# Buffers taken ahead of their loads, and the squares of the memory moved, in a one-core decoder layer

## The chip, the cores and the metric

The kernel runs on one core of one Trainium2 chip, in one launch. The metric is the device time of an execution in microseconds (us); where several were timed, it is their median. The profile is that of one execution; its times start with its span.

## The reference

One layer of a hybrid decoder: 512 tokens of width 1024, and a memory of 256 tokens of the same width, all in float32.

```python
x = x + 0.5 * swiglu(rms_norm(x, norm_ffn1_w), ffn1_w_in, ffn1_w_out)      # inner width 2816
x = x + hybrid_mixer(rms_norm(x, norm_mix_w), ..., rel_bias, w_out_mix)    # 16 SSD heads in 4 groups beside 8 attention heads
x = x + memory_cross_attention(rms_norm(x, norm_cross_w), rms_norm(mem, norm_mem_w), w_cq, w_ck, w_cv, w_co)
x = x + 0.5 * swiglu(rms_norm(x, norm_ffn2_w), ffn2_w_in, ffn2_w_out)
return rms_norm(x, norm_final_w)
```

Three things in it concern the change. `rms_norm(mem, ...)` needs the sum of squares of each memory token. The attention heads add a bias that is looked up from `rel_bias` by the bucket of the distance of two tokens. The SSD heads end in a norm over each group of 256 channels.

## The kernel before

**Matmuls.** A float32 factor is split into a rounded part and the remainder (`wh` and `wl` for weights, names in `h` and `l` for activations); ScalarE makes the first (L155), VectorE the second (L156), and TensorE multiplies three pairs of parts. A weight tile `wr` comes by a transfer on SP's queue into one of six buffers, is split into one of three pairs of buffers, and is then multiplied. Some weight blocks are summed on the way: a transfer on POOL's queue adds a second block to a `wr` that has landed.

**The first feed-forward.** Both feed-forwards use a scheme of block products with sums (seven products where eight would be plain). The inner width is worked through in three thirds (`THIRDS`: 8, 8 and 6 tiles of 128). In each third, `ffn_quads` makes gate and up projections: a quad (`quad`, L240) computes two inner tiles by seven products and ends in the gated tile `th`. `block_tiles` then makes from `th` the block tiles `g` (`g11`, `s31`, `s24`, `g`), six large buffers and two small ones a quad. `out_blocks` (L1266) multiplies a third's tiles by the second weight matrix, again in seven products, `oa`, `oe` and `ob`. The first third has four quads' worth of tiles, the second four, the last three. The activations' block sums `xs` stay in their buffers through all of it.

**Buffers.** Nearly all tiles come from one pool: `s2` gives a large buffer (128 x 512, 55 of them) or, for tiles of at most 256 columns, a small one (16). A buffer that was used before can be written once all who used it are done.

**The order of the work.** The program is written by an `Order` object with a virtual clock `od.t`, which each matmul moves on by its own length and nothing else moves. Dense work (a list of generators) is emitted in turn; chains (`od.spawn`) are steps that are put in between when the virtual clock has reached their time, and each `yield n` in a chain asks for its next step `n` us of matmul time later. SP and POOL execute in the order so written. For TensorE, VectorE and ScalarE a planner orders the instructions by its own estimate of when each could start, with the order written as priority; `behind(...)` ties an instruction after another on its engine. The planner also gives each transfer of SP and ScalarE one of eight counters in turn; a transfer waits until the last one on its counter has landed.

**Around the change.** `ffn1` calls `at_out(ti)`, which is `beside`, when it begins with the output products of third `ti`:

```python
        if ti == 0:
            od.spawn(lambdas())
        elif ti == 1:
            od.spawn(memory_squares())
        elif ti == 2:
            od.spawn(prepare())
            od.spawn(memory_in(hm), 1.0)
```

`memory_squares` loads the memory by token (`memt`, four tiles, L1013) and squares them on ScalarE into `msq` (L1017). `prepare` loads the one-hot buckets `hot` (L609), multiplies them by `rel_bias` (`prel`), copies the result back into `hot` (L620) and sends it, on ScalarE's queue, to the table `rel_d` in device memory (L623), and from there to `rel_z` (`expand_bias`, L629). `memory_in` loads the memory by channel (`mem`, four tiles of two, L1024) and splits it into `hm` for the keys of the cross-attention (L159, L160). Right after the last third, x is transposed back (`pxf`), and the keys (`pck`) begin.

In the mixer, `group` runs once for each of the four SSD groups as a chain. Near its end it sums squares with TensorE (`pn`), takes the root on POOL (`ncol`, L357), halves it on VectorE (`rh`, L990), and after `W["gn"]` calls `row_of`, which builds two diagonal matrices on POOL (`ndiag`, L368). After `W["gr"]` a matmul with ones (`nrow`) makes the row by which `y` is multiplied.

Of the kernel before, what the change touches and what calls it, by code (L numbers as in the profile page):

```python
# [13 lines left out]
AF = mybir.ActivationFunctionType  # L14
# [3 lines left out]
P = 128  # L18
T = 512
D = 1024  # L20
KT = D // P
NF = 22
MEM = 256
# [6 lines left out]
NUM_BUCKETS = 32  # L30
# [5 lines left out]
LEAD = 4  # L36

W = {"h0": 3.4, "hs": 3.3, "hv": 2.08, "hp": 6.75}
W |= {"g0": 8.28, "gc": 0.75, "gx": 0.92, "gb": 2.59, "gs": 0.51, "gt": 2.0, "gd": 6.9, "gy": 0.38, "gq": 11.8, "gn": 5.0, "gr": 3.0}
W |= {"c0": 4.97, "cs": 3.0, "ct": 4.82}  # L40

SPLIT, AHEAD = 5, 2
# [58 lines left out]
def body(tc, a, dbg=None):  # L101
    nc = tc.nc
# [12 lines left out]
    def nm(s):  # L115
        uid[0] += 1
        return f"{s}_{uid[0]}"

    def s2(s, dt=F32, shape=(P, T)):
        if math.prod(shape[1:]) <= T // 2:  # L120
            return sp.tile(list(shape), dt, tag="s1", name=nm(s), bufs=NHALF)
        return sp.tile(list(shape), dt, tag="s2", name=nm(s))
# [4 lines left out]
    def small(s, n, bufs=None):  # L127
        return tiny.tile([P, n], F32, tag=s, name=nm(s), bufs=bufs)
# [4 lines left out]
    def aux(s, shape=(P, T)):  # L133
        return aux_p.tile(list(shape), F32, tag="aux", name=nm(s))
# [5 lines left out]
    last, start, last_sum, recent, newest, newest_mm = [], [], [], [], [], []  # L140
    V, S, G = nc.vector, nc.scalar, nc.gpsimd
    od = Order()

    def mm(out, w, x, start, stop):
        od.t += (1 if w.dtype == R32 else 4) * (x.free_size() + 8) / 2400
        newest_mm[:] = [nc.tensor.matmul(out, w, x, start=start, stop=stop).ins]  # L146
# [16 lines left out]
    def split(s, src, scale=None, half=False, n=T):  # L163
        if half:
            both = s2(s, R32, (P, 2, T // 2))
            hi, lo = both[:, 0], both[:, 1]
        else:
            hi, lo = s2(s + "h", R32, (P, n)), s2(s + "l", R32, (P, n))
        last[:] = [i.ins for i in split_into(hi, lo, src, scale)]
        return hi, lo  # L170
# [12 lines left out]
    @contextmanager  # L183
    def behind(ins):
        with ExitStack() as after:
            for i in ins:
                after.enter_context(tc.issue_after(i))
            yield

    H = T // 2  # L190
# [359 lines left out]
    def beside(ti):  # L550
        if ti == 0:
            od.spawn(lambdas())
        elif ti == 1:
            od.spawn(memory_squares())
        elif ti == 2:
            od.spawn(prepare())
            od.spawn(memory_in(hm), 1.0)
# [17 lines left out]

    od.spawn(st1.finish(rows=0.0), 18.0)
    od.add(ffn1(h1, wa_s, beside, square, fin1))


# [6 lines left out]
    def lambdas():  # L586
        lamv = cp.tile([P, 4, 64], F32, name="lamv")
        nc.sync.dma_start(lamv, a["lam"].partition_broadcast(P))
        yield 8.0
        lamp = small("lamp", 64, bufs=2)  # L590
        lsum = small("lsum", 2, bufs=1)
        for j in range(2):
            V.tensor_tensor(lamp, lamv[:, 2 * j, :], lamv[:, 2 * j + 1, :], ALU.mult)
            V.reduce_sum(lsum[:, j : j + 1], lamp, axis=AX.X)
        yield 4.0
        lexp = small("lexp", 2, bufs=1)
        G.tensor_tensor(lexp, euler[:, 0:1].to_broadcast([P, 2]), lsum, ALU.pow)
        yield 4.0
        V.tensor_tensor(nlam, lexp[:, 1:2], lexp[:, 0:1], ALU.subtract)
        V.tensor_scalar(nlam, nlam, -LAMBDA_INIT, None, ALU.add)  # L600
        V.tensor_scalar(wsub, par[:, C_SUBLN : C_SUBLN + 1], 1.0 - LAMBDA_INIT, None, ALU.mult)
        V.tensor_scalar(dskh, par[:, C_DSKIP : C_DSKIP + 8], 0.5, None, ALU.mult)

    def prepare():
        rel_sb = small("rel_sb", 8, bufs=1)[:NUM_BUCKETS]
        nc.sync.dma_start(rel_sb, a["rel_bias"])
        hot = [s2("hot", shape=(NUM_BUCKETS, H)) for _ in range(2)]
        for i in range(2):
            nc.sync.dma_start(hot[i], a["hot"][:, i * H : (i + 1) * H])  # L609
        rel_far = small("rel_far", 64, bufs=1)[:8]  # L610
        V.memset(rel_far, MASKED)
        yield 9.0
        prel = aux("prel", (8, T))
        for i in range(2):
            mm(prel[:, i * H : (i + 1) * H], rel_sb, hot[i], True, True)
        for c in range(T, RW, 64):
            S.dma_start(rel_d[:, c : c + 64], rel_far)
        yield 1.5
        for i in range(2):
            S.activation(hot[i][:8], prel[:, i * H : (i + 1) * H], AF.Copy, scale=-8.0)  # L620
        yield 2.0
        for i in range(2):
            S.dma_start(rel_d[:, i * H : (i + 1) * H], hot[i][:8])  # L623
        yield 6.0
        for hd in range(2):
            expand_bias(S, hd)

    def expand_bias(queue, hd):
        queue.dma_start(rel_z[hd, :, :RW], rel_d[hd : hd + 1].to_broadcast([P, RW]))  # L629
# [377 lines left out]

    msq = small("msq", 4, bufs=1)

    def memory_squares():  # L1010
        mt = [s2("memt") for _ in range(4)]
        for j in range(4):
            nc.sync.dma_start(mt[j], a["memt"][j])  # L1013
        yield 12.0
        for j in range(4):
            with behind(list(recent)):
                S.activation(mt[j], mt[j], AF.Square, accum_out=msq[:, j : j + 1])  # L1017
            yield 4.0

    def memory_in(dst):  # L1020
        mem = []
        for k in range(0, KT, 2):
            mem.append(s2("mem2", shape=(P, 2, MEM)))
            nc.sync.dma_start(mem[-1], a["memT"][k : k + 2].rearrange("k p m -> p k m"))  # L1024
        yield 9.0
        for k in range(KT):
            mk = mem[k // 2][:, k % 2]
            with behind(recent):
                dst.append(split("hm", mk, par[:, C_MEM + k : C_MEM + k + 1], True))
            yield 2.0  # L1030
        both = small("nboth", 4, bufs=2)[:, :2]
        V.tensor_tensor(both, msq[:, :2], msq[:, 2:], ALU.add)
        yield from st_mem.from_sums(both, 10.0)
# [477 lines left out]
```

## Time and profile before

| | |
|---|---|
| median of 3 runs | 1342.84 us (1339.92 to 1343.74) |
| the profiled execution | 1341.54 us, span 1339.8 us |
| granted TensorE clock, mean | 0.988 |
| instructions | 20126 |
| busy: TensorE, VectorE, ScalarE, POOL | 97%, 74%, 53%, 9% of the span |
| moved by transfers | 236.34 MB, mean 176 GB/s |

In the profile PE is TensorE's matmuls and PEld its weight loads, DVE is VectorE, ACT ScalarE, POOL GpSimd, SP the engine that issues most transfers; SPq or ACTq marks a queue's own work, issuing and waiting. L155 is line 155 of the kernel. A row of a timeline has start and length in us, engine, line, operation, output and inputs, count, and in brackets the idle time before it with what ended it. A row of waits has who waited, for whom, and then total, number and longest in us. In the tables by stretches each row has the stretch, its length, each engine's busy time with its instructions in brackets, the granted clock as a share of full speed, the busy share of the transfer engines, and GB/s.

### The profile page before, as it was taken

The page shows a single profiled execution, that of the slowest core. Times are in us where ns is not written, and L with a number is a line of the kernel's source. Part 1 is how long each engine was busy: PE and PEld are TensorE (multiplying, and loading weights), DVE is VectorE, ACT ScalarE, POOL GpSimd, SP SyncE. Part 2 cuts the span into 40 slices and gives each one's busy share as a digit, 9 for nine tenths or more (in the row PEclk, how much of TensorE's full clock was granted, in tenths as well). Part 3 has the DMA queues.
Part 4 walks back from the last instruction along what each step waited for, and adds up shares of the span by engine and source line. Part 5 has one row for each costly group of instructions (what it writes and reads, how often), then busy time and mean ns, then how long its engine had stood idle before and what let it go on. Part 6 is the DMA issues. An engine that isn't in the chain of part 4 may idle for free.

```text
span 1339.8 us, 20126 instructions
## 1 busy us (share of the span) xinstructions
PE 1303.0 (97%) x7724; PEld 1131.8 (84%) x7724; DVE 985.9 (74%) x1564; ACT 709.6 (53%) x1192; POOL 124.0 (9%) x143
## 2 busy tenths in 40 slices
PE   9999997999899999989999999999999999999996
PEld 7898996898697778777788878888889989989995
DVE  7988785787786577637867868645588877877886
ACT  6554553455564464526655547334456545554564
POOL 0001010000020001010110311120001100000001
PEclk9999998999899999999999999999999999999999
DMA  7658765775794634673375647766148876656662
GB/s 269 167 168 209 184 159 172 208 185 137 228 310 158 180 83 95 212 209 111 81 179 189 151 142 227 228 172 190 47 127 222 212 228 180 188 192 180 186 207 86
DMA packets 70129, 236.34 MB, mean 176 GB/s; under 512 B 8257, under 2 KB 9761, under 8 KB 69681
## 3 DMA queue, kind: packets, MB, share of 16 engines
q1 hardware_dynamic: 54352, 183.20, 40.7%
q0 software_dynamic: 12880, 44.62, 19.2%
q10 hardware_dynamic: 2800, 7.23, 1.5%
q8 instruction: 61, 1.00, 0.3%
q14 instruction: 36, 0.29, 0.1%
HBM read 232.87 MB, written 50.91 MB: 212 GB/s over the span
## 4 chain that ended last, share of the span: by engine, by line
PE 91%; DMA 3%; DVE 3%; ACT 2%; issue 1%; POOL 0%; ACTq 0%; SPq 0%; POOLq 0%; DVEq 0%
PE qb L240 12%; PE pm L146 9%; PE qe L240 8%; PE qa L240 8%; PE pxbc L146 7%; PE ob L1266 6%; PE oe L1266 4%; PE oa L1266 4%; PE pq L146 3%; PE pk L146 3%; PE pcq L146 3%; PE pz L146 3%; PE pv L146 3%; PE pck L146 2%; PE pcv L146 2%; PE pg L146 2%
## 5 line engine op out<-in xcount | busy, mean ns | idle before, releaser
L155 ACT ACTIVATE wh<-wr 128x1024 fp32r<-128x1024 f32 (+1 forms) x329 | 334.9, 1021 | 381.8 <-issue 63.1
L156 DVE TENSOR_TENSOR wl<-wr,wh 128x1024 fp32r<-128x1024 f32 (+1 forms) x329 | 385.4, 1174 | 159.7 <-ACT wh L155 157.0
L146 PE MATMUL pxbc<-hnh,wh 128*128 128x512 f32 x128 | 52.2, 408 | 0.0
L146 PE MATMUL pxbc<-hnh,wl 128*128 128x512 f32 x128 | 50.3, 393 | 0.0
L146 PE MATMUL pxbc<-hnl,wh 128*128 128x512 f32 x128 | 50.1, 392 | 0.0
L763 ACT ACTIVATE ec<-ec,mn 128x512 f32<-128x512 f32 (+3 forms) x64 | 35.5, 557 | 24.1 <-DVE mn L762 24.1
L240 PE MATMUL qe<-s31h,wl 128*128 128x256 f32 x152 | 43.1, 283 | 0.0
L240 PE MATMUL qa<-h11h,wh 128*128 128x256 f32 x152 | 43.1, 283 | 0.0
L240 PE MATMUL qb<-s24h,wh 128*128 128x256 f32 x152 | 43.0, 283 | 0.0
L240 PE MATMUL qb<-s24l,wh 128*128 128x256 f32 x152 | 43.0, 283 | 0.0
L240 PE MATMUL qb<-s24h,wl 128*128 128x256 f32 x152 | 43.0, 283 | 0.0
L240 PE MATMUL qa<-hmh,wh 128*128 128x256 f32 x152 | 43.0, 283 | 0.0
L240 PE MATMUL qa<-hml,wh 128*128 128x256 f32 x152 | 43.0, 283 | 0.0
L240 PE MATMUL qa<-hmh,wl 128*128 128x256 f32 x152 | 43.0, 283 | 0.0
L240 PE MATMUL qe<-s24h,wh 128*128 128x256 f32 x152 | 43.0, 283 | 0.0
L240 PE MATMUL qe<-s24l,wh 128*128 128x256 f32 x152 | 43.0, 283 | 0.0
L240 PE MATMUL qe<-s24h,wl 128*128 128x256 f32 x152 | 43.0, 283 | 0.0
L240 PE MATMUL qb<-hmh,wh 128*128 128x256 f32 x152 | 43.0, 283 | 0.0
L240 PE MATMUL qb<-hml,wh 128*128 128x256 f32 x152 | 43.0, 283 | 0.0
L240 PE MATMUL qb<-hmh,wl 128*128 128x256 f32 x152 | 43.0, 283 | 0.0
L240 PE MATMUL qa<-h11h,wl 128*128 128x256 f32 x152 | 43.0, 283 | 0.0
L240 PE MATMUL qa<-h11l,wh 128*128 128x256 f32 x152 | 43.0, 283 | 0.0
(448 smaller groups left out, 4190.8 us busy)
## 6 DMA issues: line engine op xcount, KB each, us to landing
wr<-in_f2q SPq DMA_DIRECT2D x44, 512.0 KB, 4.4
wr<-in_f1q SPq DMA_DIRECT2D x40, 512.0 KB, 4.5
wr<-in_f1b SPq DMA_DIRECT2D x30, 512.0 KB, 5.2
isum<-in_f2q SPq DMA_DIRECT2D x22, 512.0 KB, 5.9
wr<-isum SPq DMA_DIRECT2D x22, 512.0 KB, 4.8
wsum<-in_f2b SPq DMA_DIRECT2D x20, 512.0 KB, 5.9
wr<-wsum SPq DMA_DIRECT2D x20, 512.0 KB, 4.4
wr<-in_f1q POOLq DMA_DIRECT2D x16, 512.0 KB, 7.5
```

The lines of the kernel that those rows point to most:

```text
L146: newest_mm[:] = [nc.tensor.matmul(out, w, x, start=start, stop=stop).ins]
L155: S.activation(hi, src, AF.Copy),
L156: V.tensor_tensor(lo, src, hi.bitcast(F32), ALU.subtract),
L240: newest_mm[:] = [nc.tensor.matmul(out, a_[:, wc], b_, start=first and f == 0 and kp == 0 and j == 0, stop=kp == n - 1 and j == 2, skip_gr ...
L763: S.activation(ec[:, :n], ec[:, :n], AF.Exp, bias=mn, scale=-1.0, accum_out=sm[c][:, i : i + 1])
L1266: newest_mm[:] = [nc.tensor.matmul(ps, a_[:, ts], b_[:, ws], start=first and k == 0 and j == 0, stop=k == n - 1 and j == 2, skip_group_che ...
```

## The change

It has two parts. The first concerns the memory loads. `memory_squares` becomes `early`, still spawned at the second third's output products. It waits 40 us of matmul time, takes the four `memt` buffers, waits 20 more, loads them, and squares them 14 later, one each 1.0 (before: load at once, squares from 12 on, one each 4.0, tied behind the latest weight split; now not tied). It then takes the four buffers of `mem` and the two of `hot`, ahead of `memory_in` and `prepare`, which use them where they took them before, and drop them with `clear()`. The second part changes two distances in `group`: from the root to the diagonals ("gn") 5.0 becomes 1.5, and from the diagonals to the row's matmuls ("gr") 3.0 becomes 5.3.

```diff
-... "gq": 11.8, "gn": 5.0, "gr": 3.0}
+... "gq": 11.8, "gn": 1.5, "gr": 5.3}
...
         elif ti == 1:
-            od.spawn(memory_squares())
+            od.spawn(early())
...
     def prepare():
         rel_sb = small("rel_sb", 8, bufs=1)[:NUM_BUCKETS]
         nc.sync.dma_start(rel_sb, a["rel_bias"])
-        hot = [s2("hot", shape=(NUM_BUCKETS, H)) for _ in range(2)]
         for i in range(2):
             nc.sync.dma_start(hot[i], a["hot"][:, i * H : (i + 1) * H])
...
             S.dma_start(rel_d[:, i * H : (i + 1) * H], hot[i][:8])
+        hot.clear()
         yield 6.0
...
-    def memory_squares():
+    mem, hot = [], []
+
+    def early():
+        yield 40.0
         mt = [s2("memt") for _ in range(4)]
+        yield 20.0
         for j in range(4):
             nc.sync.dma_start(mt[j], a["memt"][j])
-        yield 12.0
+        yield 14.0
         for j in range(4):
-            with behind(list(recent)):
-                S.activation(mt[j], mt[j], AF.Square, accum_out=msq[:, j : j + 1])
-            yield 4.0
+            S.activation(mt[j], mt[j], AF.Square, accum_out=msq[:, j : j + 1])
+            yield 1.0
+        mem.extend(s2("mem2", shape=(P, 2, MEM)) for _ in range(KT // 2))
+        hot.extend(s2("hot", shape=(NUM_BUCKETS, H)) for _ in range(2))

     def memory_in(dst):
-        mem = []
         for k in range(0, KT, 2):
-            mem.append(s2("mem2", shape=(P, 2, MEM)))
-            nc.sync.dma_start(mem[-1], a["memT"][k : k + 2].rearrange("k p m -> p k m"))
+            nc.sync.dma_start(mem[k // 2], a["memT"][k : k + 2].rearrange("k p m -> p k m"))
         yield 9.0
...
             yield 2.0
+        mem.clear()
```

More of the change, by code (lines that the diff above doesn't have):

```diff
@@ L38 @@
 W = {"h0": 3.4, "hs": 3.3, "hv": 2.08, "hp": 6.75}
-W |= {"g0": 8.28, "gc": 0.75, "gx": 0.92, "gb": 2.59, "gs": 0.51, "gt": 2.0, "gd": 6.9, "gy": 0.38, "gq": 11.8, "gn": 5.0, "gr": 3.0}
+W |= {"g0": 8.28, "gc": 0.75, "gx": 0.92, "gb": 2.59, "gs": 0.51, "gt": 2.0, "gd": 6.9, "gy": 0.38, "gq": 11.8, "gn": 1.5, "gr": 5.3}
 W |= {"c0": 4.97, "cs": 3.0, "ct": 4.82}
```

## The prediction

> **What bounds the kernel now.** I read the page first, then TensorE's waits, then each feed-forward stage alone in the table by stretches, then what SP and ScalarE waited for there.
>
> ```profile
> span 1339.8 us, 20126 instructions
> ## 1 busy us (share of the span) xinstructions
> PE 1303.0 (97%) x7724; PEld 1131.8 (84%) x7724; DVE 985.9 (74%) x1564; ACT 709.6 (53%) x1192; POOL 124.0 (9%) x143
> ```
>
> ```profile
> PE oa L1266 <- ACT wh L155: 7.9, 3, 4.0
> PE oe L1266 <- ACT wh L155: 7.7, 2, 5.5
> ```
>
> TensorE is the bound, with 1339.8 - 1303.0 = 36.8 us idle. A change that leaves the matmuls alone can win only idle time and time at a lowered clock. The two largest waits, 15.6 us, are in `out_blocks` (L1266). The next table (stretch, its length, busy time of PE, PEld, DVE, ACT, POOL, granted clock, DMA share, GB/s) sets its three runs in the first feed-forward side by side: the thirds with four, four and three quads. The third row is the quads between the last two.
>
> ```profile
> 94.16:132.47 38.31, 38.31 (x170) 31.45 (x170) 33.11 (x40) 19.87 (x23) 3.44 (x4) 1.00 0.77 208
> 213.16:266.20 53.04, 44.14 (x172) 34.78 (x171) 33.81 (x39) 22.64 (x31) 4.26 (x5) 0.87 0.73 212
> 266.20:326.58 60.38, 60.38 (x505) 60.38 (x504) 49.53 (x58) 32.52 (x40) 5.12 (x6) 1.00 0.74 182
> 326.58:370.06 43.48, 35.85 (x134) 26.32 (x133) 30.85 (x45) 23.93 (x45) 1.74 (x2) 0.88 0.59 181
> ```
>
> The first two do the same matmuls. One takes 38.31 us without an idle moment, the other 53.04 with 8.90 idle and a mean clock of 0.87. So stage A (213 to 266) loses 53.04 - 38.31 = 14.7 us. Stage B (326 to 370) has three quads; a later third of that size shows each of its seven products:
>
> ```profile
> 1075.19 4.08 PE oa L1266 x18
> ```
>
> ```profile
> 332.14 1.02 PE L146 MATMUL prel<-hot,rel_sb 32*8 32x256 f32 x4
> ```
>
> Seven by 4.08 is 28.6; with `prepare`'s matmuls of 1.0 it is 29.6. Stage B loses 43.5 - 29.6 = 13.9 us. The quads lose nothing. Together 28.6 us are to be had, and why they are lost is in SP's own waits (from 189 to 217 us, then from 304 to 336) and in when its weight loads go out:
>
> ```profile
> SPq L1013 <- DVE qe L300: 14.8, 1, 14.8
> SPq L1013 <- DVE g11l L156: 8.0, 1, 8.0
> SPq L1013 <- DVE c L307: 2.5, 1, 2.5
> SPq L1247 <- DVE wl L156: 2.2, 1, 2.2
> SPq L1013 <- DVE s24l L156: 0.2, 1, 0.2
> ```
>
> ```profile
> SPq L1247 <- DMA rel_d<-hot: 17.2, 1, 17.2
> SPq L1024 <- DMA wr<-in_f1b: 5.3, 1, 5.3
> ```
>
> ```profile
> 78.97 33.80 SPq L1247 DMA_DIRECT2D wr<-in_f1b  x10
> ...
> 216.88 30.31 SPq L1247 DMA_DIRECT2D wr<-in_f1b  x10
> ...
> 313.51 36.43 SPq L1247 DMA_DIRECT2D wr<-in_f1b  x10
> ```
>
> SP issues in the order written. At L1013 (`memt`) it stood 14.8 + 8.0 + 2.5 + 0.2 = 25.5 us for buffers, released by the last quad's `u2`, `p5` and `s24` and by the block split that follows it, and A's ten remaining weight loads were behind it. In the clean third their first goes out at 78.97, 15.2 us ahead of the stage; in A at 216.88, 3.7 us after its start: 18.9 us late. The code's count agrees: the pool has 55 large buffers. At the end of a third of four quads it holds 24 for `xs` (six a pair), 24 for `g` (six a quad), one row, three copies of a quad and two unsplit sums: 54. Four `memt` do not fit. With three quads it is 48, and four more make 52.
>
> In B the loads begin at 313.51 in good time, but then one stands 17.2 us for the landing of `rel_d<-hot`, and the rest behind it. No data joins the two. SP's and ScalarE's transfers take eight counters in turn, and one waits for the last transfer on its counter; the order is the planner's, which thought the weights late since it held `hot` and `mem` behind the last quad's buffers. ScalarE shows the same order:
>
> ```profile
> 333.21 0.64 ACT L620 ACTIVATE hot<-prel 8x256 f32<-8x256 f32 x2 [0.26 <-PE prel L146]
> 333.61 0.63 ACTq L623 DMA_DIRECT2D rel_d<-hot  x2
> 335.27 1.22 ACTq L629 DMA_DIRECT2D rel_z<-rel_d  x2
> 336.53 0.63 ACT L155 ACTIVATE wh<-wr 128x512 fp32r<-128x512 f32 x1 [2.68 <-issue]
> ```
>
> The split that TensorE needs at 332 stands behind the bias work, though its load was out at 313.51.
>
> **The change, part by part.** *Memory by token.* Four loads, four squares and their buffers leave stage A. `early` takes buffers 40 us after its start (A's 38.3 and some 2 us of quads), loads at 60 and squares from 74. The pool is then far from full. SP no longer stands in front of A's weights; the clean third is the model, so A becomes 38.3. **Gain 14.7**, between 0 (SP stands as long elsewhere) and 14.7. What is late next in A is nothing: VectorE's 33.81 us stay beside the clean third's 33.11. In the quads the moved work costs:
>
> ```profile
> L1013 SPq DMA_DIRECT2D memt<-in_memt x4: 327/328/328, 204.9 to 216.5; - x4
> L1017 ACT ACTIVATE memt<-memt x4: 615/616/621, 235.1 to 251.2; 128x512 f32<-128x512 f32 x4
> ```
>
> SP spends 4 x 0.33 = 1.3 us, ScalarE 4 x 0.62 = 2.5 us where it is busy 32.5 of 60.4: hidden. Without that cover 2.5 us come back. The squares also lose their place behind the weight splits; one of 0.62 ahead of a split is covered by the spare `wh` buffers.
>
> *`mem` and `hot`.* The same six loads stay at the start of B, but their buffers were set aside in the last quad. SP loses L1024's wait of 5.3 us or part of it, and the planner sees loads and weights early: ScalarE gets B's split ahead of `hot`, and the counters that `rel_d<-hot` holds meet later transfers. Queued behind them on SP are B's ten loads and then the keys' weights. What is late next is VectorE: 30.85 us of work for 29.6 of matmuls.
>
> ```profile
> DVE th L449 <- ACT gate L447: 1.1, 1, 1.1
> DVE gate L446 <- PE qb L240: 0.7, 1, 0.7
> ```
>
> ```profile
> 369.41 1.43 DVE L1277 SCALAR_TENSOR_TENSOR x<-ob,col,x 128x512 f32<-128x512 f32 x2 [0.15 <-PE ob L1266]
> ```
>
> Its two waits at the start remain, and its last update, 1.4 us, falls after the last matmul: 30.85 + 1.1 + 0.7 - 1.4 = 31.3 us is its floor in B. I add some 1.7 for hand-overs and take 33 (an estimate): **gain 43.5 - 33 = 10.5**, between 0 (the old order stays) and 13.9 (memory splits slip behind the stage).
>
> What such a remainder does to the clock is one question more:
>
> ```profile
> 355.69 0.79 PE L1266 MATMUL oe<-wh,s24h 128*128 128x512 f32 x1 [2.17 <-ACT wh L155]
> ...
> 360.00:361.00 1.00, 1.00 (x4) 0.71 (x4) 0.00 (x0) 0.17 (x1) 0.00 (x0) 0.50 1.01 385
> ```
>
> After a wait of 2.17 us the granted clock is still 0.50 at 360: about 6 us at half speed, 3 us lost. One such gap in B makes it 36 and the gain 7.5. The Trainium skill ("TensorE: Matmul & The Clock Gate", Part 1) says that the clock falls after at least one idle window of about 3.4 us. By that rule alone a remainder of short gaps would cost no clock and the sum would stay 1316.3; by the row above it would be 1319.3. The trace disagrees with the rule as stated: 2.17 us were enough here.
>
> *Group norm's row.* The wait between sum and diagonals falls from 5.0 to 1.5, that between diagonals and row matmuls rises from 3.0 to 5.3: the row is asked 1.2 us of matmul time sooner.
>
> ```profile
> 842.63 1.04 POOL L368 TENSOR_TENSOR ndiag<-ident,cl 128x512 fp32r<-128x512 f32 x1
> ```
>
> ```profile
> 844.91 0.62 PE L146 MATMUL nrow<-ndiag,ones_r 128*128 128x512 f32 x2
> ```
>
> This is the last and tightest of the four groups: the diagonals end at 843.67, and the row 1.2 us sooner would start at 843.71, still after them. POOL stands some 2 us in front of its later transfers, which fill blocks read much later. If POOL came late by the whole step, TensorE would wait in its place: four groups by 1.2 us make +4.8. The gain is bounded by 1.2 us of the last group, if the output projection waited for it. I take **0**.
>
> **Sum.** 14.7 + 10.5 + 0 = 25.2. The profiled execution took 1341.54 (span 1339.8), 1.3 under the median of 1342.84. 1341.5 - 25.2 = **1316.3 us**.
>
> **The rivals.** *Only A is mended.* ScalarE still meets `prel` and the landing of `rel_d` before B's splits, or the counters fall so that a weight load again waits for them. For it: neither the matmuls nor the transfers of `prepare` are moved. Against: the planner's reason for the order goes. 1341.5 - 14.7 = 1326.8. Chance 0.15.
>
> *SP's standing moves into the quads.* `memt` now stands among their weight loads, and SP runs ahead of TensorE, so it may reach buffers taken only at 40 us before they are free. For it: the lead of 15 us above. Against: A's sums are freed as its products end. Then A's 14.7 is paid in the quads: 1341.5 - 10.5 = 1331.0. Chance 0.07.
>
> *Slower: the reserved buffers starve the last quad.* If the pool holds four more than I count, `mem` leaves too few for that quad's copies and sums, and these wait until memory splits free one.
>
> ```profile
> 352.62 1.30 ACT L159 ACTIVATE hm<-mem,par 128x256 fp32r<-128x256 f32 x3
> ```
>
> From the end of that quad, 326.6, to the split that frees the first `mem` buffer it is 26 us, plus 3 of lowered clock as above. 1341.5 - 14.7 + 29 = 1355.8. It decides once 52 is short by four, so that the pool of 55 is passed. Chance 0.04. That nothing changes, since something else holds the weights back in A and B, gets 0.03.
>
> **How the numbers follow.** The forecast has 0.71, its own range 1312.9 (B's whole 13.9) to 1319.3 (one half-clock gap). To hold the time 8 times in 10 the range goes from 1312 up to 1328 and takes in the case of A alone; the last three cases, 0.14, stay out. About 0.3% (4 us) is what a measurement of this kernel can tell from no change. Faster by more: 0.71 + 0.15 + 0.07 = 0.93, lowered to 0.92; the same 0.03; slower 0.05.
>
> **What would show it.** Right: no SP wait at `memt`, A near 38.3 at clock 1.00; in B a split `wh` ahead of `hot` on ScalarE, no SP wait on `rel_d`, VectorE over 90% busy; 1303.0 of PE time falls to some 1291, since matmuls at half clock go. Wrong: a new PE wait on `wh` between 266 and 327, a wait of `u2` or `p5` for a buffer, or stage B unchanged.

## The result, and the profile after

The changed kernel takes **1328.09 us** (median of 4 runs, 1326.03 to 1329.7), the kernel before 1342.76 on the same chip: a ratio of 0.9893, interval 0.9871 to 0.9916. The forecast was 1316.3, so 14.7 us came instead of 25.2 (medians). The profiled execution took 1329.7 us, 11.8 less than the one before (1341.54); that the medians fell by just what was forecast for A alone is chance.

The page, for the span and each engine's busy time:

```profile
span 1327.5 us, 20129 instructions
...
PE 1298.4 (98%) x7724; PEld 1129.5 (85%) x7724; DVE 987.1 (74%) x1564; ACT 708.5 (53%) x1192; POOL 123.2 (9%) x143
```

TensorE's idle time fell from 36.8 to 1327.5 - 1298.4 = 29.1 us. Its busy time fell by 4.6, not by the 12 that were forecast. The table by stretches shows where, with stage A, the quads behind it and stage B:

```profile
213.10:253.05 39.95, 38.91 (x172) 31.56 (x171) 33.15 (x40) 20.03 (x23) 3.41 (x4) 1.00 0.75 213
253.05:313.50 60.45, 60.45 (x505) 60.41 (x505) 48.93 (x58) 35.10 (x48) 5.12 (x6) 1.00 0.76 198
313.50:357.52 44.02, 35.97 (x134) 26.74 (x134) 30.77 (x45) 23.90 (x45) 1.74 (x2) 0.84 0.59 179
```

Stage A went from 53.04 to 39.95, clock 1.00. The quads, which now hold the loads and squares of `memt`, stayed at 60.4. Stage B stayed: 43.48 before, 44.02 now. TensorE's waits, SP's waits and SP's timeline say the same:

```profile
PE oa L1270 <- ACT wh L155: 4.4, 2, 4.0
...
PE oe L1270 <- ACT wh L155: 2.3, 1, 2.3
```

```profile
SPq L1251 <- DMA rel_d<-hot: 17.2, 1, 17.2
```

```profile
264.54 1.85 SPq L1017 DMA_DIRECT2D memt<-in_memt  x4
...
287.50 2.96 SPq L1251 DMA_DIRECT2D wr<-in_f1b  x2
...
290.99 1.05 SPq L608 DMA_DIRECT2D hot<-in_hot  x2
292.14 3.94 SPq L1027 DMA_DIRECT2D mem<-in_memT  x4
300.50 36.60 SPq L1251 DMA_DIRECT2D wr<-in_f1b  x10
```

SP stands at `memt` for 0.3 us in place of 25.5. But it still stands 17.2 us for `rel_d<-hot`, and ScalarE's timeline at the start of B shows the order of before:

```profile
314.50 1.06 ACT L447 ACTIVATE gate<-gate 128x1024 f32<-128x1024 f32 x1 [2.67 <-DVE gate L446]
...
320.20 0.64 ACT L619 ACTIVATE hot<-prel 8x256 f32<-8x256 f32 x2 [0.27 <-PE prel L146]
320.60 0.62 ACTq L622 DMA_DIRECT2D rel_d<-hot  x2
322.25 1.21 ACTq L629 DMA_DIRECT2D rel_z<-rel_d  x2
323.50 0.63 ACT L155 ACTIVATE wh<-wr 128x512 fp32r<-128x512 f32 x1 [2.67 <-issue]
```

ScalarE idles 2.67 us ahead of the gate and 2.67 ahead of that split, although the ten weight loads began at 300.50, some 13 us before the stage. So the weights were on their way in time. What is late is the place of the split. (Two of the stage's weight loads, at 287.50, and their splits are in the quad already; "the first split" below is the first of the ten weights that go out at 300.50.)

### The profile page after: what moved, and what is told of

Its sections match the earlier page's. It is cut to its first block, busy times and chain, and to the rows that moved or that the text cites. A ratio compares the mean times of both kernels' runs of the same rounds, so it can differ in the third digit from the quotient of the medians.

```text
span 1327.5 us, 20129 instructions
## 1 busy us (share of the span) xinstructions
PE 1298.4 (98%) x7724; PEld 1129.5 (85%) x7724; DVE 987.1 (74%) x1564; ACT 708.5 (53%) x1192; POOL 123.2 (9%) x143
## 4 chain that ended last, share of the span: by engine, by line
PE 91%; DVE 3%; DMA 2%; ACT 1%; issue 1%; POOL 0%; ACTq 0%; POOLq 0%; DVEq 0%
PE qb L240 12%; PE pm L146 10%; PE qe L240 8%; PE qa L240 8%; PE pxbc L146 7%; PE ob L1270 6%; PE oe L1270 4%; PE oa L1270 4%; PE pq L146 4%; PE pk L146 3%; PE pcq L146 3%; PE pz L146 3%; PE pv L146 3%; PE pck L146 2%; PE pa L146 2%; DMA wr<-in_f1b 2%
```

## The experiments

Each ratio is to the kernel before on the same chip. On the experiments' chips that one took 1339.89 to 1341.43 us, 1.3 to 2.9 less than on the changed kernel's, and the times expected below are too high by so much. A and B are the lengths of the two stages in the profiled execution, by the rows shown below each experiment or by the same table where no row is shown.

| kernel | median us | ratio, interval | A | B |
|---|---|---|---|---|
| before | 1342.76 | | 53.04 | 43.48 |
| the changed kernel | 1328.09 | 0.9893, 0.9871 to 0.9916 | 39.95 | 44.02 |
| e1_memt_alone | 1326.77 | 0.9906, 0.9890 to 0.9921 | 38.60 | 41.98 |
| e2_row_alone | 1340.25 | 1.0002, 0.9992 to 1.0012 | 51.99 | 41.80 |
| e3_aside_alone | 1341.06 | 1.0003, 0.9992 to 1.0014 | 52.43 | 43.38 |
| e4_loads_early | 1319.01 | 0.9833, 0.9819 to 0.9847 | 38.35 | 31.56 |
| e5_prepare_early | 1319.13 | 0.9842, 0.9830 to 0.9855 | 40.39 | 34.14 |
| e6_rel_d_on_pool | 1325.51 | 0.9886, 0.9872 to 0.9899 | 41.18 | 40.68 |
| e7_hot_early | 1327.46 | 0.9901, 0.9884 to 0.9918 | 42.08 | 41.86 |
| e8_mem_early | 1323.97 | 0.9876, 0.9862 to 0.9889 | 40.97 | 39.18 |
| e9_memt_on_pool | 1334.05 | 0.9949, 0.9934 to 0.9965 | 46.57 | 41.41 |
| e10_rel_z_on_pool | 1327.20 | 0.9897, 0.9876 to 0.9917 | 39.31 | 42.23 |
| e11_loads_later | 1317.97 | 0.9832, 0.9817 to 0.9847 | 38.34 | 32.09 |
| e12_minimal | 1320.42 | 0.9843, 0.9830 to 0.9857 | 38.25 | 32.14 |

One of e4's five executions took 7275.27 us, at a clock of 1.00; its ratio leaves that one out, and no run here says why it was so long.

**The change taken apart.** e1 moves memory by token and does nothing else:

```diff
     def memory_squares():
+        yield 40.0
         mt = [s2("memt") for _ in range(4)]
+        yield 20.0
...
-        yield 12.0
+        yield 14.0
...
-            with behind(list(recent)):
-                S.activation(mt[j], mt[j], AF.Square, ...)
-            yield 4.0
+            S.activation(mt[j], mt[j], AF.Square, ...)
+            yield 1.0
```

> The kernel before with memory by token alone: its four loads and squares move from the start of stage A into the quads behind it; no buffers of `mem` and `hot` are set aside, the group norm's waits stay as before. Theory (setting buffers aside does nothing, all of the change's gain is stage A's): stage A near 40 us at clock 1.00 against 53.0, stage B unchanged at 43 to 44, SP's 17.2 us wait for rel_d still there, time 1328 to 1330, level with the whole change. Rival (setting aside or the group's row brings part of the gain): 1331 or more. Rival (they cost something, which hides a part of the gain in the whole change): under 1326.

e2 changes the two numbers of the group norm only:

```diff
-... "gn": 5.0, "gr": 3.0}
+... "gn": 1.5, "gr": 5.3}
```

> The kernel before with the group norm's row alone asked 1.2 us of matmul time sooner (waits 1.5 and 5.3 in place of 5.0 and 3.0). Theory (row and diagonals were hidden): 1342.8, no difference beyond 1 us. Rival (the row was late for the output projection, or comes before its diagonals now): 1341.6 or less, by 1.2 us of the last group, or up to 1347.6, by 1.2 us in each of four groups.

e3 only takes the buffers ahead of their loads, at 78 us of matmul time after the start of A's output products:

```diff
         elif ti == 1:
             od.spawn(memory_squares())
+            od.spawn(aside(), 78.0)
...
+    def aside():
+        mem.extend(s2("mem2", shape=(P, 2, MEM)) for _ in range(KT // 2))
+        hot.extend(s2("hot", shape=(NUM_BUCKETS, H)) for _ in range(2))
+        yield 0.0
```

> The kernel before with the buffers of `mem` and `hot` alone taken in the last quad, ahead of their loads; memory by token and the group norm stay as before. Theory (the planner binds a buffer to a tile at the tile's first write, not where the tile is named, so nothing moves): 1342.8 within 1 us, stage A 53, stage B 43.5, SP's 17.2 us wait for rel_d there as before. Rival (my prediction's step: buffers taken early let the planner put weights ahead of the bias work): stage B 33, time near 1332.

e1's interval, 0.9890 to 0.9921, overlaps that of the whole change, 0.9871 to 0.9916. e2 and e3 are level with the kernel before to 0.15%. So the gain is memory by token's, as far as these intervals tell. (B is 41.98 in e1, not the 43 to 44 expected, but e2 has 41.80 with the order of before: B scatters by some 2 us.) The row of e3's waits, and its stages in the table by stretches:

```profile
SPq L1254 <- DMA rel_d<-hot: 17.2, 1, 17.2
```

```profile
215.53:267.96 52.43, 43.99 (x171) 34.77 (x170) 34.01 (x39) 22.51 (x31) 4.26 (x5) 0.87 0.74 214
328.50:371.88 43.38, 35.65 (x132) 26.16 (x131) 30.59 (x45) 23.70 (x44) 1.74 (x2) 0.88 0.60 181
```

Nothing moved in e3, and nothing could: with the buffers taken ahead, the built program has on each of the five engines the same instructions in the same order as the one before (none of some 12,000 differs). Taking a buffer is a name in the code; the planner meets it only where something is first written to it, and that is the load, which stands where it stood.

**What mends stage B.** e4 therefore moves the loads too, out of `prepare` and `memory_in` to where the buffers are taken. The bias work and the splits of `mem` stay in B:

```diff
     def early():
...
         hot.extend(s2("hot", shape=(NUM_BUCKETS, H)) for _ in range(2))
+        for i in range(2):
+            nc.sync.dma_start(hot[i], a["hot"][:, i * H : (i + 1) * H])
+        for k in range(0, KT, 2):
+            nc.sync.dma_start(mem[k // 2], a["memT"][k : k + 2].rearrange("k p m -> p k m"))
```

> The changed kernel with the six loads of `hot` and `mem` issued in the last quad, right where their buffers are taken; the bias work and the splits of `mem` stay at the start of stage B. Theory (the first write binds the buffer; only now does the planner see the weights early): B's weight loads stand ahead of the bias work's transfers in SP's order, no SP wait of 17 us for rel_d, a split wh ahead of hot on ScalarE, stage B 31 to 35 in place of 44.0, time 1316 to 1321. Rival (the place of the loads doesn't matter, B is set by ScalarE's bias work or by VectorE's 30.8 us with its waits): stage B 41 to 44, 1326 to 1329. Rival (the loads starve the last quad of buffers): PE waits for u2 or p5 ahead of stage B, 1330 or more.

Its stages, SP's timeline, and ScalarE's at the start of B (at 314.54):

```profile
215.45:253.80 38.35, 38.35 (x170) 31.45 (x169) 32.35 (x38) 19.92 (x23) 3.16 (x4) 1.00 0.80 220
...
314.54:346.10 31.56, 30.29 (x133) 23.70 (x132) 29.81 (x45) 23.45 (x45) 1.71 (x2) 1.00 0.76 223
```

```profile
285.91 0.89 SPq L1023 DMA_DIRECT2D hot<-in_hot  x2
286.89 1.93 SPq L1025 DMA_DIRECT2D mem<-in_memT  x4
288.91 2.53 SPq L1251 DMA_DIRECT2D wr<-in_f1b  x2
...
301.46 30.92 SPq L1251 DMA_DIRECT2D wr<-in_f1b  x10
```

```profile
314.62 0.63 ACT L155 ACTIVATE wh<-wr 128x512 fp32r<-128x512 f32 x1 [1.82 <-PE qb L240]
315.95 1.06 ACT L447 ACTIVATE gate<-gate 128x1024 f32<-128x1024 f32 x1 [0.70 <-DVE gate L446]
317.31 0.63 ACT L155 ACTIVATE wh<-wr 128x512 fp32r<-128x512 f32 x1 [0.30 <-PE oa L1270]
...
320.04 1.07 ACT L155 ACTIVATE wh<-wr 128x1024 fp32r<-128x1024 f32 x1
```

Stage B is 31.56 with the clock at 1.00, and VectorE is busy 29.81 of it. The ten weight loads begin 314.54 - 301.46 = 13.1 us before the stage, as in the changed kernel (313.5 - 300.5 = 13.0). On the chip the loads of hot and mem came only some 6 us earlier against the stage. What differs is ScalarE's order: three splits at 0.1, 2.8 and 5.5 us into the stage, where the changed kernel has its first at 323.50 - 313.5 = 10.0. ScalarE uses time for them in which it idled before.

e5 goes on and puts all of `prepare` into the last quad:

```diff
-            od.spawn(prepare())
...
     def early():
...
+        yield from prepare()
```

> The kernel e4_loads_early, and `prepare` whole (its loads, matmuls, copies and the transfers of rel_d and rel_z) in the last quad in place of stage B's start. Theory (B's 43.5 us came from the planner's late weights, and e4 has mended that): nothing more to win than the bias work itself, 1.0 us of matmuls and 1.3 us of copies, stage B 30 to 31.5, time 1316 to 1320, level with e4. Rival (the bias work in B still costs several us, by its transfers and its place on ScalarE): 1314 or less. Rival (ScalarE's standing for rel_d now meets the last quad): PE waits before stage B, 1321 or more.

Level with e4 in the total; in the profiled execution B was longer than the 30 to 31.5 expected, for one wait on VectorE's part of a split:

```profile
315.39:349.53 34.14, 30.62 (x128) 24.58 (x127) 29.64 (x45) 23.14 (x42) 1.71 (x2) 0.95 0.66 188
```

```profile
336.50 0.50 PE L1270 MATMUL ob<-wl,s31h 128*128 128x512 f32 x1 [3.52 <-DVE wl L156]
```

So the bias work in B costs nothing that shows once the splits are in front. Why that split came late here was not tried.

e11 goes the other way. It loads later than the changed kernel, not earlier:

```diff
     def prepare():
+        yield 12.0
         rel_sb = small("rel_sb", 8, bufs=1)[:NUM_BUCKETS]
...
     def memory_in(dst):
+        yield 7.0
         for k in range(0, KT, 2):
...
-        yield 9.0
+        yield 4.0
```

> The changed kernel with the loads of `mem` issued 7 us and those of `hot` and the bias work 12 us of matmul time later (the splits of `mem` 2 us later), behind the first weight loads of stage B in SP's order; no load is earlier than in the changed kernel. Theory (what spoils B is that loads whose buffers come free late stand ahead of the weight loads in SP's order, so that the planner plans the weights and their splits late; either direction out of it mends B): three splits wh before or at the start of B as in e4, stage B 31 to 34, 1316 to 1320. Rival (buffers must be filled early, as in e4): stage B 39 or more, 1324 or more. Rival (bias work and memory's splits moved later now meet the keys): B mended, and PE waits of 2 us or more for hm or prel behind it, 1320 to 1326.

```profile
212.81:251.15 38.34, 38.34 (x170) 31.45 (x169) 32.91 (x39) 19.91 (x23) 3.41 (x4) 1.00 0.79 221
311.91:344.00 32.09, 30.75 (x132) 23.48 (x131) 29.74 (x45) 22.57 (x43) 1.70 (x2) 1.00 0.72 206
```

```profile
285.83 17.55 SPq L1253 DMA_DIRECT2D wr<-in_f1b  x5
303.44 1.96 SPq L1029 DMA_DIRECT2D mem<-in_memT  x4
305.99 2.98 SPq L1253 DMA_DIRECT2D wr<-in_f1b  x2
...
309.69 0.91 SPq L609 DMA_DIRECT2D hot<-in_hot  x2
```

```profile
311.99 0.63 ACT L155 ACTIVATE wh<-wr 128x512 fp32r<-128x512 f32 x1 [1.82 <-PE qb L240]
```

B is 32.09, with the first split 0.1 us into the stage. So it is not that `hot` and `mem` have to be early. What the three orders of SP differ in is where the six loads stand among B's twelve weight loads: in the changed kernel between the second and the third, in e4 ahead of the first, in e11 behind the fifth (`mem`) and the seventh (`hot`). The splits were late with the first of these orders alone. e12 is e11's delays on e1, without the set-aside buffers and the group norm's numbers (its edit is those of e1 and e11 together):

> The kernel before with memory by token as in the changed kernel and the loads and waits of e11_loads_later, but without the buffers set aside and without the group norm's new waits. Theory (setting aside and the row do nothing, here neither): stage A 38 to 42, stage B 31 to 34, time 1316 to 1320, level with e11. Rival (buffers taken ahead matter once the loads are out of the way): stage B 36 or more, 1322 or more.

```profile
314.13:346.27 32.14, 30.78 (x132) 23.48 (x131) 29.72 (x45) 22.53 (x43) 1.71 (x2) 1.00 0.70 199
```

The set-aside buffers and the row do nothing here that shows either: the intervals of e11 and e12 overlap (e12's 1320.42 is 0.4 us above the range expected). e4, e5, e11 and e12 all beat the changed kernel by some 0.5 to 0.6%, with intervals apart from its own.

**Which part of the order in B costs.** The wait that stands out in the profile is SP's 17.2 us. e6 takes it away by sending rel_d on another queue, whose transfers don't use the eight counters:

```diff
-            S.dma_start(rel_d[:, i * H : (i + 1) * H], hot[i][:8])
+            nc.gpsimd.dma_start(rel_d[:, i * H : (i + 1) * H], hot[i][:8])
```

> The changed kernel with the two transfers rel_d<-hot on GpSimd's queue in place of ScalarE's, so that they hold none of the eight counters of the hardware queues; the loads of `hot` and `mem` stay in stage B. Theory (two costs in B, the counter and ScalarE's order): SP's 17.2 us wait for rel_d is gone, rel_z no longer stands ahead of the first split on ScalarE, which still follows the copies of hot, so that PE's first wait in B falls from 4.0 us to some 1.5 and the later ones of 1.2 and 2.3 go: stage B 32 to 37 in place of 44, 1316 to 1322. Rival (the counter is harmless, the late loads do it): stage B 41 or more, 1326 to 1329.

```profile
315.44:356.12 40.68, 35.84 (x132) 26.27 (x131) 30.65 (x45) 23.48 (x44) 2.85 (x4) 0.87 0.58 175
```

```profile
322.06 0.64 ACT L619 ACTIVATE hot<-prel 8x256 f32<-8x256 f32 x2 [0.27 <-PE prel L146]
322.60 0.61 ACT L155 ACTIVATE wh<-wr 128x512 fp32r<-128x512 f32 x1
```

My expectation of 32 to 37 was wrong. The wait is gone, TensorE's first wait fell from 4.0 to 1.25, and B still takes 40.68. The seven profiled kernels that kept this order on ScalarE and the counter (before, the changed one, e1, e2, e3, e7, e9) have B between 41.41 and 44.02, so the gain is 0.7 to 3.3 us by one profile of e6, and the total's interval overlaps that of the changed kernel. The first split still stands behind the copies of `hot`, 7.2 us into the stage. e10 keeps SP's wait and takes only rel_z away from in front of the split:

```diff
         for hd in range(2):
-            expand_bias(S, hd)
+            expand_bias(nc.gpsimd, hd)
```

> The changed kernel with the two transfers rel_z<-rel_d on GpSimd's queue in place of ScalarE's; rel_d<-hot stays on ScalarE's, holds its two counters, and one of them still meets an early weight load. So SP still stands for rel_d, but the first split of B no longer stands behind rel_z on ScalarE. Theory since e6 (SP's 17.2 us cost nothing, rel_z ahead of the split cost PE's first wait its 2.8 us, and the rest of B's loss is the late planned splits): SP's wait for rel_d of 10 us or more is still there, PE's first wait 1.0 to 1.5 us, stage B 39.5 to 41, level with e6, 1323 to 1326. Rival (SP's standing is what costs): stage B 43 to 44, 1326 to 1329.

```profile
SPq L1251 <- DMA rel_d<-hot: 16.8, 1, 16.8
```

```profile
315.14:357.37 42.23, 35.19 (x132) 26.27 (x131) 30.76 (x45) 23.61 (x44) 2.86 (x4) 0.88 0.60 186
```

B is inside the unchanged kernels' scatter, above the 39.5 to 41 expected. TensorE's first wait did fall, to 1.8 us, but one of 4.2 us came 20 us later, when ScalarE waited for weights that SP had sent late. So the counter and rel_z give about 2 us (42.6, the mean of the seven, less 40.68) when both go, and nothing that can be told when rel_z alone goes. The counter alone was not tried, so how they share it stays open.

e7 and e8 each move one half of e4's loads, `hot` in e7 and `mem` in e8, with the lines of e4's edit:

> The changed kernel with the two loads of `hot` alone issued in the last quad; the loads of `mem` stay in stage B. By the turn of the counters rel_d<-hot still meets an early weight load of B, and rel_z still stands ahead of the first split on ScalarE. Theory (the late loads of `mem` hold B's weights and their splits back by themselves): stage B 43 to 44, SP's wait for rel_d 17 us, PE's first wait in B 4.0 us, 1326 to 1329. Rival (the loads of hot are what holds them): stage B 31 to 36, 1316 to 1321.

> The changed kernel with the four loads of `mem` alone issued in the last quad; the loads of `hot` stay in stage B. The loads of hot still hold the planner's weights back, but by the turn of the counters rel_d<-hot now shares its two with a weight load late in B instead of an early one, and the first split stands ahead of rel_z on ScalarE. Theory (what costs is whom the counter of rel_d meets and what stands before the first split): no SP wait of 17 us, stage B 32 to 37, 1316 to 1322. Rival (a late `hot` alone is enough to spoil B): stage B 41 or more, 1326 to 1329.

```profile
316.05:357.91 41.86, 35.27 (x132) 25.89 (x131) 30.44 (x45) 23.59 (x44) 1.73 (x2) 0.88 0.60 188
```

```profile
314.90:354.08 39.18, 32.62 (x132) 24.47 (x131) 30.50 (x45) 23.74 (x44) 1.71 (x2) 0.96 0.61 178
```

e7 (the first row) has the waits of the theory, 17.2 us on SP and 4.0 on TensorE, and the time; its B is 1.1 us below the range, within the scatter. e8 (the second row) missed: SP's wait is gone and one copy of `hot` moved behind the first split, but B is 2.2 us above the range of 32 to 37 and 7.6 us longer than in e4. Either group of loads, left where it was, keeps the splits late: the first comes 9.9 us into the stage in e7 and 6.9 in e8. The planner's own estimate of the loads' start appears in no trace, so that it alone makes them late is inferred.

**Stage A's cause.** e9 leaves memory by token in A but loads it on GpSimd's queue:

```diff
-            nc.sync.dma_start(mt[j], a["memt"][j])
+            nc.gpsimd.dma_start(mt[j], a["memt"][j])
```

> The kernel before with the four loads of memory by token on GpSimd's queue in place of SP's; they stay at the start of stage A, as do the squares and the buffers. Theory (A's 14.7 us came from SP standing in front of A's weight loads): no SP wait at memt, most weight loads go out ahead of A, and only the few weight loads on GpSimd's queue stand behind memt: stage A 39 to 46, 1328 to 1336. Rival (the squares on ScalarE or the buffers that memt holds in A did it): stage A 51 to 54, 1339 to 1343.

Its stage A, GpSimd's timeline, and TensorE's wait:

```profile
213.12:259.69 46.57, 41.27 (x171) 33.15 (x170) 33.57 (x39) 22.70 (x31) 4.83 (x6) 0.93 0.69 187
```

```profile
217.22 0.54 POOL L1013 DMA_DIRECT2D memt<-in_memt  x1 [8.00 <-DVE th L449]
218.09 0.89 POOL L1286 DMA_DIRECT2D wr<-in_f1b  x1 [0.33 <-issue]
```

```profile
226.97 0.80 PE L1266 MATMUL oe<-wh,s31h 128*128 128x512 f32 x1 [5.26 <-ACT wh L155]
```

SP never waits at memt, and A falls by 6.5 us, to 0.6 above the range expected. The rest looks like the same mechanism on the other queue, though no run took it away: GpSimd stood 8.0 us for the last `memt` buffer, and the weight block that it adds went out at 218.09, five us into the stage. The squares stayed in A, and the 5.26 us are TensorE's only wait in it, so they cost nothing that shows. So 6.5 us of A's loss are shown to be SP standing in front of weights, with the squares and the buffers where they were; that the 8.3 us left above the clean third's 38.3 are GpSimd's standing is argued from these rows.

## Why the prediction was right or wrong

**Memory by token: right, its size 1.6 us too large.** The term was 14.7; the profiled executions give 53.04 - 39.95 = 13.1, and e1 alone gives 1339.89 - 1326.77 = 13.1 in the total. "What is late next in A is nothing" was a little too clean. In the ten kernels that move `memt`, A lies between 38.25 and 42.08, with a mean of 39.7; the clean third's 38.3 is their lower end. Where it is longer, TensorE waits for `g11h`, `g11l` or `s31l`; `g11h`, from which `g11l` is made, stands on ScalarE behind a weight split that waited (1.74 us in the changed kernel) for its load to land. Why that load lands late in some executions wasn't tried.

**The quads: right.** 60.38 before, 60.45 after; SP's standing did not move there.

**`mem` and `hot`: this step failed.** It read "the planner sees loads and weights early", and gave 10.5 us; the stage gave -0.5. The diagnosis of stage B held: what bounds it is the place of B's splits on ScalarE, and the price was right too. With that order gone B is 31.56 (e4) and 32.09 (e11), against 33 forecast. The floor of 31.3 was misread: of the last update's 1.4 us only 0.65 (369.41 to 370.06) lay inside the stage, which makes it 32.0, and e4's 31.56, with VectorE busy 29.81, shows that it was no floor. But the change does not touch the cause. Buffers were set aside, yet the six loads, as the prediction itself says, "stay at the start of B", and e3 shows that the program in order of instructions is then the old one. I took a line of code for a state that the planner sees, and gave its plain failure no more than the 0.15 of *Only A is mended*.

**SP's 17.2 us: overrated.** The prediction named the counter and ScalarE's order side by side. By e6 the long wait and rel_z together cost some 2 us. That leaves the rest of the 12 to the place of the splits, by subtraction; no run moved the splits alone.

**Group norm's row: right at 0.** e2 is at 1.0002. The last group's matmuls run 1.5 us behind the diagonals, as they ran 1.2 behind before:

```profile
830.17 1.04 POOL L368 TENSOR_TENSOR ndiag<-ident,cl 128x512 fp32r<-128x512 f32 x1
```

```profile
832.74 0.62 PE L146 MATMUL nrow<-ndiag,ones_r 128*128 128x512 f32 x2
```

**The rivals and the range.** *Only A is mended* came, by both of its conditions: ScalarE still meets `prel` and the landing of `rel_d` before the split, and a weight load again waits for `rel_d`. Its 1326.8 stands against 1328.09. The range's upper end, 1328.0, had 1.2 us above that rival and so no room for A's own scatter of 4 us. With both terms as measured the sum is 1341.5 - 13.1 + 0.5 = 1328.9, and the profiled execution took 1329.7.

## What to carry to other kernels

Before pricing a change to a program that a planner orders, ask which instruction of the program it moves; a buffer taken earlier, with the same first write in the same place, moves none. Where a load stands among the weight loads of a queue can decide how the planner orders another engine, even when on the chip the weights are out in time: here six loads cost 12 us between the second and the third of a stage's weights, and nothing that shows ahead of the first or further behind. The longest wait in a profile need not be the dear one: look for the engine that idles next to work that it could do, here ScalarE's 2.67 us ahead of the gate.

## What the runs showed of the hardware

ScalarE did not pass over a waiting step: in the changed kernel it idled 2.67 us in front of a split whose load had been issued long before, while rel_z ahead of it waited for rel_d. With rel_z on the other queue (e10) the split came 7.7 us into the stage and not 10.0. The Trainium skill ("TensorE: Matmul & The Clock Gate", "Architectural detail: the array is 16× 32×32, not 1× 128×128") says that ScalarE's and VectorE's queues are strictly first in, first out; these rows of ScalarE agree, and for VectorE no run here shows it.

The clock falls after waits still shorter than the 2.17 us that the prediction showed. In e7 one of 1.93 us was followed by half clock, and in e6 one of 1.25 us, right behind `prel`'s small matmuls; in e4 one of 1.27 us was not, nor in e8 one of 1.46. So the length of the wait alone doesn't decide it; what else does, no run here shows. The rows are of e7, e6 and e4:

```profile
344.66 0.50 PE L1270 MATMUL oe<-wh,s24h 128*128 128x512 f32 x1 [1.93 <-ACT wh L155]
...
347.00:348.00 1.00, 1.00 (x4) 0.81 (x3) 1.00 (x2) 0.00 (x0) 0.00 (x0) 0.50 0.75 238
```

```profile
323.27 0.50 PE L1270 MATMUL oa<-wh,g11h 128*128 128x512 f32 x1 [1.25 <-ACT wh L155]
...
325.00:326.00 1.00, 1.00 (x4) 0.35 (x2) 0.17 (x2) 0.88 (x2) 0.00 (x0) 0.50 0.78 209
```

```profile
334.56 0.50 PE L1270 MATMUL ob<-wl,s31h 128*128 128x512 f32 x1 [1.27 <-DVE wl L156]
...
337.00:338.00 1.00, 1.00 (x6) 0.84 (x5) 0.65 (x2) 0.00 (x0) 0.00 (x0) 1.00 0.92 326
```

The Trainium skill ("TensorE: Matmul & The Clock Gate", Part 1) names an idle window of about 3.4 us; as in the prediction, the measurements disagree with that as stated. The lowered clock is why B's waits cost more than their length. Between the changed kernel's B and e4's lie 44.02 - 31.56 = 12.5 us. The waits that the timeline lists are 4.02 + 0.41 + 1.17 + 2.34 = 7.9 us in the one and 1.27 in the other, 6.7 apart; the same matmuls take 35.97 us of busy time in the one, at a mean clock of 0.84, and 30.29 in the other, at 1.00, 5.7 apart.
